# Even attention: the keys' low parts in four lasting tiles, written once each, with the other half of the rows zeroed one time

## The chip, the cores and the metric

The kernel runs on one core of one Trainium2 chip. The core has five engines, each with its own in-order instruction stream: TensorE (PE, matrix products into PSUM), VectorE (DVE), ScalarE (ACT), GpSimd (POOL) and SyncE (SP, which starts most of the transfers). Weight loads of TensorE are shown as PEld. The metric is the time of one execution on the device in microseconds (us); less is better.

## The reference

A two-layer block over 512 positions and 256 context positions with 1024 channels. Layer 0 (the "even" one, the place of the change) mixes a gated chunk MLP with a differential attention of four heads; layer 1 is a windowed attention; each is followed by a SwiGLU feed-forward. Cut to the even attention:

```python
def diff_attn(q, k, v, lam):
    b, tq = q.shape[0], q.shape[1]
    tk = k.shape[1]
    s = jnp.einsum('bqhd,bkhd->bhqk', q, k).astype(jnp.float32) * ATTN_SCALE
    p = jax.nn.softmax(s, axis=-1).reshape(b, B_HEADS, 2, tq, tk)
    a = p[:, :, 0] - lam * p[:, :, 1]
    return jnp.einsum('bhqk,bkhe->bqhe', a.astype(v.dtype), v)

# even_mixer: q, k are rotated (rope); keys and values of the context are appended
k_all = jnp.concatenate([k, kc], axis=1)      # 512 + 256 = 768 keys
o = lax.map(lambda qb: diff_attn(qb, k_all, v_all, lam), q_blocks)
oc = diff_attn(qc, kc, vvc, lam)              # context queries, context keys alone
```

Each of the four heads has two components of 64 channels (the softmaxes that are subtracted) and values of 128 channels.

## The kernel before

**Precision by parts.** TensorE multiplies here in the type fp32r. To come nearer to float32, a tensor is split: its high part is the value cast to fp32r, its low part is what is left (the value less the high part). A general product is then three matmuls (`mm3`, lines 115 to 117): high x high, high x low, low x high.

**Scores by stacking.** A component has 64 channels and TensorE contracts over 128 rows, so the scores do it in two matmuls instead of three. Call a half of the 128 rows X for one component (rows 0 to 63 for the first, 64 to 127 for the second) and the other half Y. `stack_q` makes for each component a tile of queries (`qa`, `qb`) with the high part in X and the low part in Y (lines 272, 273 on ACT; line 276 on DVE, on POOL for the last head). `stack_k` makes for each component two tiles of keys: `kh` has the high part in both halves (lines 287, 288 on ACT), `kl` has the low part in both halves (line 290 on DVE, once for X and once for Y). The query tile times `kh` gives high x high and low x high, the query tile times `kl` gives high x low and low x low (lines 553 and 554: 512 columns of the sequence, 256 of the context). All four key tiles of a head come from a ring of six buffers (tag "sk"), 128 x 768 in fp32r.

**Work of a head.** `head(t)` runs three pairs of query blocks (`attend`, qp 0 to 2; the last pair are the context's queries, which see 256 keys alone). For each block and component (`softmax_diff`): score product into a PSUM tile `pw` (two such tiles), DVE's maximum (line 555), ACT's exponential `e` with its sum (line 557), then on DVE the reciprocal (561), a factor (562), the difference of the two softmaxes (563) and a small row (564). Then TensorE transposes `e` (line 575), ACT casts the high part `ath` (131), DVE subtracts the low part `atl` (132), and `mm3` multiplies with the values; ACT copies the output (587). The next head's tiles (`stack(t + 1)`) are made after a head's second pair. The head's norm runs in three steps inside the next head (sums by line 165, small operations 144 to 148 and 176, diagonal matrices by line 185 multiplied at 195, then line 620).

**The rest of the stage.** Between the attention's steps TensorE has filler work: the gated projections `gated(i)`, into a PSUM tile `pf` by `mm3`, copied out by ACT (line 596), their weights cast by ACT (89) with the low part subtracted on POOL (92). After the first two heads come four gelus on ACT (line 643, here with a table load, and a second load for the exponentials after it), and per group transposes (655), copies (656) and statistics (659, 660).

**What sets the order.** The program is written by head and by group; a scheduler orders each engine's instructions by priority and by an estimate of when operands and buffers come free. Heads 2 and 3 have a raised priority. A different number of instructions or another buffer therefore changes the order on several engines, also of lines that the change doesn't touch. The order on each engine is then fixed; at run time an engine waits for the next instruction in its row.

## Time and profile before

| what | us |
|---|---|
| runs, median | 1572.99 |
| runs, lowest to highest | 1571.8 to 1576.91 |
| the profiled execution | 1574.88 |
| its span in the profile | 1573.0 |
| TensorE busy in the span | 1514.1 |
| VectorE busy | 1073.0 |
| GpSimd busy | 826.1 |
| ScalarE busy | 727.8 |
| mean granted clock of TensorE | 0.994 |

Times in the profile run from the start of its span. In a timeline row stand the start, the duration, the engine, the line of the kernel, the operation, what is written <- what is read, the shape, and in brackets the time for which the engine was idle just before and which engine's work ended that. The first attention, with the projections between, takes the stretch from about 157 to 350 us.

### The profile page before, as it was taken

Reading aid. Unit: us, or ns where it says so; the run is one execution under the profiler, and the core shown is the slowest. Engines: PE = TensorE matmul, PEld = TensorE weight load, DVE = VectorE, ACT = ScalarE, POOL = GpSimd, SP = SyncE. Lnnn points to the kernel's source line nnn. Section 1 sums busy time; section 2 is a strip of 40 time slices with the busy share of each in tenths; the row PEclk is TensorE's granted clock in tenths of the full one; section 3 lists DMA queues with packets and bytes.
Section 4 is the critical chain, followed back from the end, with each engine's and each line's share of the span. In section 5 each row is a group of like instructions: output and inputs, shape, how many; then the busy total and the mean of one; then the engine's idle time right before and its main releaser. Section 6 shows DMA issues by size and latency. Waiting matters only on the chain.

```text
span 1573.0 us, 24994 instructions
## 1 busy us (share of the span) xinstructions
PE 1514.1 (96%) x9563; PEld 1352.0 (86%) x9563; DVE 1073.0 (68%) x1938; ACT 727.8 (46%) x1490; POOL 826.1 (53%) x558
## 2 busy tenths in 40 slices
PE   6999987999999999999999999999999999999998
PEld 4776876889999999999999988777869889999997
DVE  3720788765697787888786486765667966666665
ACT  2422677553553333333333354555645644444444
POOL 0464211050347777777776544531314399898982
PEclk9999999999999999999999999999999999999999
DMA  9835100033223333344542212200224133333301
GB/s 331 311 131 201 45 8 1 1 134 134 68 74 121 114 95 128 128 150 165 167 157 85 79 47 61 68 28 15 68 95 173 54 104 103 104 100 108 95 21 54
DMA packets 53416, 162.26 MB, mean 103 GB/s; under 512 B 6193, under 2 KB 8625, under 8 KB 45617
## 3 DMA queue, kind: packets, MB, share of 16 engines
q1 hardware_dynamic: 46240, 135.37, 25.7%
q10 hardware_dynamic: 7056, 25.30, 5.0%
q8 instruction: 75, 1.23, 0.3%
q14 instruction: 45, 0.36, 0.1%
HBM read 158.55 MB, written 2.10 MB: 102 GB/s over the span
## 4 chain that ended last, share of the span: by engine, by line
PE 85%; DVE 10%; ACT 3%; issue 1%; DMA 0%; DVEq 0%; SPq 0%; ACTq 0%
PE pw L115 12%; PE pw L116 12%; PE pw L117 11%; PE pb L116 8%; PE pb L117 8%; PE pb L115 8%; PE pf L115 4%; PE pf L116 4%; PE pf L117 4%; PE pb L1635 2%; PE pb L1624 2%; PE pf L370 2%; PE pw L1586 1%; PE pw L1594 1%; DVE t L49 1%
## 5 line engine op out<-in xcount | busy, mean ns | idle before, releaser
L116 PE MATMUL pw<-ax,w 128*128 128x384 f32 (+2 forms) x740 | 237.0, 321 | 3.5 <-DVE ax L49 2.2
L115 PE MATMUL pw<-ax,w 128*128 128x384 f32 (+2 forms) x740 | 235.9, 321 | 3.6 <-DVE q L49 1.9
L117 PE MATMUL pw<-ax,w 128*128 128x384 f32 (+2 forms) x740 | 236.4, 320 | 0.1
L785 DVE SCALAR_TENSOR_TENSOR xT<-pb,mod,xT 128x512 f32<-128x512 f32 (+3 forms) x204 | 143.2, 708 | 129.3 <-PE pb L117 128.8
L92 POOL TENSOR_TENSOR w<-raw,w 128x512 fp32r<-128x512 f32 (+1 forms) x76 | 115.4, 1526 | 219.0 <-ACT w L89 196.3
L49 POOL TENSOR_TENSOR w<-raw,w 128x512 fp32r<-128x512 f32 x122 | 185.0, 1531 | 48.8 <-ACT w L49 48.7
L49 POOL TENSOR_TENSOR w<-t,w 128x512 fp32r<-128x512 f32 x99 | 148.7, 1505 | 55.7 <-ACT w L49 55.7
L115 PE MATMUL pb<-hh,w 128*128 128x512 f32 x480 | 171.4, 357 | 1.2 <-DVE xT L785 1.2
L117 PE MATMUL pb<-hh,w 128*128 128x512 f32 x480 | 171.7, 358 | 0.4 <-DVE w L49 0.4
L116 PE MATMUL pb<-hh,w 128*128 128x512 f32 x480 | 171.3, 357 | 0.0
L115 PE MATMUL pw<-T,w 128*128 128x384 f32 (+1 forms) x508 | 156.6, 310 | 2.5 <-DVE hs L991 1.2
L116 PE MATMUL pw<-T,w 128*128 128x384 f32 (+1 forms) x508 | 157.0, 310 | 1.2 <-DVE T L132 1.2
L117 PE MATMUL pw<-T,w 128*128 128x384 f32 (+1 forms) x508 | 157.0, 310 | 0.0
L116 PEld LDWEIGHTS pw<-ax,w 128*128 128x128 f32 x740 | 140.8, 190 | 10.4 <-DVE ax L477 3.1
L115 PEld LDWEIGHTS pw<-ax,w 128*128 128x128 f32 x740 | 140.0, 190 | 10.6 <-DVE q L49 2.7
L115 PE MATMUL pf<-ax,w 128*128 128x256 f32 (+2 forms) x428 | 140.7, 329 | 3.9 <-ACT f L596 2.8
L117 PEld LDWEIGHTS pw<-ax,w 128*128 128x128 f32 x740 | 140.7, 190 | 3.3 <-DVE w L954 0.4
L116 PE MATMUL pf<-ax,w 128*128 128x256 f32 (+2 forms) x428 | 139.6, 326 | 0.0
L117 PE MATMUL pf<-ax,w 128*128 128x256 f32 (+2 forms) x428 | 139.5, 326 | 0.0
L49 POOL TENSOR_TENSOR hh<-hs,hh 128x768 fp32r<-128x768 f32 (+1 forms) x42 | 77.3, 1842 | 94.7 <-ACT hh L49 70.7
L49 POOL TENSOR_TENSOR w<-rawo,w 128x512 fp32r<-128x512 f32 x59 | 103.8, 1759 | 28.6 <-ACT w L49 28.6
L240 DVE SCALAR_TENSOR_TENSOR junk<-ar,cb 128x1024 bf16<-128x1024 f32 x64 | 105.7, 1651 | 0.0
(412 smaller groups left out, 3909.2 us busy)
## 6 DMA issues: line engine op xcount, KB each, us to landing
raw<-ffn_in SPq DMA_DIRECT2D x44, 1024.0 KB, 5.1
ar<-ada SPq DMA_DIRECT2D x24, 1024.0 KB, 6.8
ar<-ada ACTq DMA_DIRECT2D x48, 512.0 KB, 3.6
rawo<-ffn_out SPq DMA_DIRECT2D x88, 256.0 KB, 3.0
raw<-odd_out SPq DMA_DIRECT2D x28, 256.0 KB, 2.7
raw<-qk SPq DMA_DIRECT2D x16, 256.0 KB, 7.9
raw<-uv SPq DMA_DIRECT2D x16, 256.0 KB, 2.7
raw<-even_out SPq DMA_DIRECT2D x8, 512.0 KB, 3.9
```

Source lines behind the costliest of these rows:

```text
L49: self.tail[key] = fn(*args, **kw)
L92: eng.tensor_tensor(lo, raw, hi.bitcast(F32), ALU.subtract)
L115: mm(out, s[0], m[0], start=start, stop=False, **kw)
L116: mm(out, s[0], m[1], start=False, stop=False, **kw)
L117: return mm(out, s[1], m[0], start=False, stop=stop, **kw)
L240: return self.nc.vector.scalar_tensor_tensor(junk, t, 1.0, self.cb[who], ALU.mult, ALU.mult, accum_out=self.acc[who][:, col:col + 1])
L370: nc.tensor.matmul(ps[32 * q:32 * q + 32, :w], cst[:, k, :], t[:, w * q:w * q + w], start=k == 0, stop=k == KT - 1, skip_group_check=True)
L785: ins = self.nc.vector.scalar_tensor_tensor(h, ps[:, r], self.modcol(l, j, m, who), h, ALU.mult, ALU.add)
L1586: nc.tensor.matmul(ps[:, st:en], Q, K[g][p][:, b0 * P:b1 * P], start=p == 0, stop=p == 1, skip_group_check=True)
L1594: last = nc.tensor.matmul(ps[:, en:en + TC], Q, K[g][p][:, TX:], start=p == 0 and not edge, stop=p == 1, skip_group_check=True)
L1624: last = nc.tensor.transpose(pt[:, x * P:(x + 1) * P], es[2 * (x % 2) + x // 2][:, kb * P:(kb + 1) * P], self.ident)
L1635: nc.tensor.matmul(po[64 * h:64 * h + 64, :], V[vb][:, 64 * g:64 * g + 64], t[:, h * TC:h * TC + TC], start=kb == 0, stop=kb == nb - 1, sk ...
```

## The change

`stack_k` no longer makes `kl` for itself. Four tiles for low parts are made once, two sets of two (one for each component); heads 0 and 2 use the first set, 1 and 3 the second. The half Y of each is set to zero on POOL once, before the first head; `stack_k` then has DVE write the low part to X alone. So eight of sixteen subtractions (line 290) are gone and four memsets of 64 x 768 are added. `kh` has a ring of three buffers of its own (tag "kh"). Of the score, the product low x low is no longer contained. The number and shapes of the matmuls are the same; the tiles take 3,072 bytes more of each partition (21,504 for 18,432).

```diff
-    def stack_k(self, k, pool, T, tag, bufs):
+    def stack_k(self, k, pool, T, tag, bufs, lows):
         nc = self.nc
         out = []
-        for X, Y in ((slice(0, 64), slice(64, 128)), (slice(64, 128), slice(0, 64))):
+        for X, Y, kl in zip((slice(0, 64), slice(64, 128)), (slice(64, 128), slice(0, 64)), lows):
             kh = pool.tile([P, T], F32R, name=self.uid("kh"), tag=tag, bufs=bufs)
-            kl = pool.tile([P, T], F32R, name=self.uid("kl"), tag=tag, bufs=bufs)
             nc.scalar.copy(kh[X], k[X])
             nc.scalar.copy(kh[Y], k[X])
-            for Z in (X, Y):
-                nc.vector.tensor_tensor(kl[Z], k[X], kh[X].bitcast(F32), ALU.subtract)
+            nc.vector.tensor_tensor(kl[X], k[X], kh[X].bitcast(F32), ALU.subtract)
             out.append((kh, kl))
         return out
@@
+        lows = [[Ra.tile([P, TA], F32R, name=f"kl{i}{c}") for c in range(2)] for i in range(2)]
+        for i in range(2):
+            nc.gpsimd.memset(lows[i][0][64:128].bitcast(F32), 0.0)
+            nc.gpsimd.memset(lows[i][1][0:64].bitcast(F32), 0.0)
+
         def stack(t):
             return (self.stack_q(qk[t], Ra, TA, "sq", 3, eng=nc.gpsimd if t == 3 else nc.vector),
-                    self.stack_k(qk[4 + t], Ra, TA, "sk", 6))
+                    self.stack_k(qk[4 + t], Ra, TA, "kh", 3, lows[t % 2]))
```

Lines 291 to 597 of before are two less in the changed kernel, those from 598 on three more. In what follows a name with a number is one buffer or one use of it. The order on POOL differs in the four memsets alone; on ACT, DVE and PE it differs inside the first attention, and is the same after it.

The first place is ACT while head 1's first context block is under way (before 196.68 to 203.58 us in the trace): `kh` with the numbers 1828 is head 2's key tile. Before:

```order
127 L287 CAST kh_1540<-f_105_578 64x768
128 L288 CAST kh_1540<-f_105_578 64x768
129 L273 ACTIVATE qb_1529<-f_103_574 64x768
130 L272 ACTIVATE qa_1822<-f_138_883 64x768
131 L557 ACTIVATE e_1571,sa_1566<-pw_1567,sa_1565 128x256
132 L557 ACTIVATE e_1577,sa_1566<-pw_1573,sa_1565 128x256
133 L131 CAST ath_1502<-pb_1497 128x512
134 L287 CAST kh_1828<-f_140_887 64x768
135 L288 CAST kh_1828<-f_140_887 64x768
136 L596 COPY f_368_2039<-pf_2040 128x512
```

After:

```order
127 L286 CAST kh_1542<-f_105_578 64x768
128 L287 CAST kh_1542<-f_105_578 64x768
129 L273 ACTIVATE qb_1533<-f_103_574 64x768
130 L286 CAST kh_1828<-f_140_887 64x768
131 L287 CAST kh_1828<-f_140_887 64x768
132 L272 ACTIVATE qa_1822<-f_138_883 64x768
133 L555 ACTIVATE e_1571,sa_1566<-pw_1567,sa_1565 128x256
134 L555 ACTIVATE e_1577,sa_1566<-pw_1573,sa_1565 128x256
135 L131 CAST ath_1506<-pb_1501 128x512
136 L594 COPY f_362_2035<-pf_2036 128x512
```

The two copies into `kh_1828` moved ahead of two exponentials.

The second place is PE in head 1's context pair (before about 227 to 229 us): the products of lines 553 and 554 into `pw`, and the last one that reads the first key tile of head 1, whose buffer head 2's second key tile takes. Before:

```order
948 L115 MATMUL pb_1651<-ath_1687,vhi_1290 128x256
949 L116 MATMUL pb_1651<-atl_1688,vhi_1290 128x256
950 L117 MATMUL pb_1651<-ath_1687,vlo_1291 128x256
951 L115 MATMUL pb_1651<-ath_1687,vhi_1294 128x256
952 L116 MATMUL pb_1651<-atl_1688,vhi_1294 128x256
953 L117 MATMUL pb_1651<-ath_1687,vlo_1295 128x256
954 L165 MATMUL pb_1705<-ones,sq_1601 128x128 x2
955 L575 MATMUL pb_1776<-ident_100,e_1737 128x128
956 L554 MATMUL pw_1854<-kh_1540,qb_1529 128x256
957 L554 MATMUL pw_1854<-kl_1541,qb_1529 128x256
958 L554 MATMUL pw_1867<-kh_1534,qa_1528 128x256
959 L554 MATMUL pw_1867<-kl_1535,qa_1528 128x256
```

After:

```order
948 L552 MATMUL pw_1850<-kh_1542,qb_1533 128x256
949 L552 MATMUL pw_1850<-kl_1323,qb_1533 128x256
950 L115 MATMUL pb_1651<-ath_1687,vhi_1290 128x256
951 L552 MATMUL pw_1863<-kh_1538,qa_1532 128x256
952 L552 MATMUL pw_1863<-kl_1322,qa_1532 128x256
953 L116 MATMUL pb_1651<-atl_1688,vhi_1290 128x256
954 L117 MATMUL pb_1651<-ath_1687,vlo_1291 128x256
955 L115 MATMUL pb_1651<-ath_1687,vhi_1294 128x256
956 L116 MATMUL pb_1651<-atl_1688,vhi_1294 128x256
957 L117 MATMUL pb_1651<-ath_1687,vlo_1295 128x256
958 L165 MATMUL pb_1705<-ones,sq_1601 128x128 x2
959 L573 MATMUL pb_1776<-ident_100,e_1737 128x128
```

The products `pw_1867` (now `pw_1863`) moved ahead of five products with the values, of the sums of line 165 and of one transpose.

The third place is PE at the first score products of head 3 (before about 272 to 276 us). Before:

```order
1138 L575 MATMUL pb_2347<-ident_100,e_2293 128x128
1139 L575 MATMUL pb_2347<-ident_100,e_2316 128x128
1140 L553 MATMUL pw_2471<-kh_2390,qb_2379 128x512
1141 L554 MATMUL pw_2471<-kh_2390,qb_2379 128x256
1142 L553 MATMUL pw_2471<-kl_2391,qb_2379 128x512
1143 L554 MATMUL pw_2471<-kl_2391,qb_2379 128x256
1144 L115 MATMUL pf_2896<-ax_311,w_2887 128x512
```

After:

```order
1137 L573 MATMUL pb_2343<-ident_100,e_2312 128x128
1138 L573 MATMUL pb_2343<-ident_100,e_2289 128x128
1139 L573 MATMUL pb_2343<-ident_100,e_2312 128x128
1140 L115 MATMUL pf_2888<-ax_311,w_2879 128x512
1141 L116 MATMUL pf_2888<-ax_312,w_2879 128x512
1142 L117 MATMUL pf_2888<-ax_311,w_2879 128x512
1143 L115 MATMUL pf_2888<-ax_313,w_2879 128x512
```

The filler into `pf_2896` (now `pf_2888`) stood behind the second component's score product; now sixteen of its matmuls stand ahead of it.

## Prediction

> **What bounds the kernel now.** I read the page's engine shares and the chain of work first, then a table by windows, then the waits and the timelines of TensorE (PE), VectorE (DVE) and ScalarE (ACT) where the table shows PE not full.
>
> ```profile
> PE 1514.1 (96%) x9563; PEld 1352.0 (86%) x9563; DVE 1073.0 (68%) x1938; ACT 727.8 (46%) x1490; POOL 826.1 (53%) x558
> PE 85%; DVE 10%; ACT 3%; issue 1%; DMA 0%; DVEq 0%; SPq 0%; ACTq 0%
> ```
>
> PE is the bound nearly everywhere. The change touches the first attention only, so the windows of that stage and of what follows count (window, its length, then busy time of PE, weight loads, DVE, ACT and GpSimd (POOL), granted clock, DMA):
>
> ```profile
> 150.00:350.00 200.00, 181.65 (x1099) 157.26 (x1098) 152.10 (x368) 127.51 (x244) 43.38 (x24) 0.97 0.12 38
> 350.00:425.00 75.00, 75.00 (x440) 74.17 (x438) 40.41 (x99) 31.95 (x68) 21.48 (x15) 1.00 0.31 108
> 225.00:250.00 25.00, 17.46 (x88) 13.82 (x87) 21.22 (x59) 19.29 (x35) 3.09 (x2) 0.80 0.00 0
> ```
>
> From 150 to 350 us PE is idle for 200 - 181.65 = 18.35 us; nothing that changes there can win more than that plus the slow clock. From 350 on PE is full, so what has been won or lost by then is carried to the end. The worst stretch is 225 to 250: PE idle for 7.5 us, DVE busy for 21.2 of 25, clock 0.80. The stretch after it, PE's largest wait (sum, times, longest), its stops (start, duration, in brackets the idle time before it and what ended that) and the clock:
>
> ```profile
> 250.00:275.00 25.00, 21.71 (x143) 19.39 (x144) 20.49 (x54) 17.57 (x39) 4.60 (x3) 1.00 0.00 1
> PE pw L553 <- ACT e L557: 6.5, 5, 1.8
> 200.61 0.50 PE L553 MATMUL pw<-kh,qa 128*128 128x512 f32 x1 [1.37 <-ACT e L557]
> 203.74 0.39 PE L115 MATMUL pf<-ax,w 128*128 128x256 f32 x1 [1.33 <-ACT f L596]
> 231.60 0.39 PE L554 MATMUL pw<-kh,qb 128*128 128x256 f32 x1 [2.51 <-ACT e L557]
> 241.94 0.47 PE L115 MATMUL pb<-ath,vhi 128*128 128x256 f32 x1 [1.54 <-ACT ath L131]
> 244.24 0.79 PE L553 MATMUL pw<-kh,qa 128*128 128x512 f32 x1 [1.84 <-ACT e L557]
> 271.77 0.47 PE L553 MATMUL pw<-kh,qa 128*128 128x512 f32 x1 [1.66 <-ACT e L557]
> 274.22 0.47 PE L553 MATMUL pw<-kh,qb 128*128 128x512 f32 x1 [0.96 <-ACT e L557]
> 314.69 0.38 PE L115 MATMUL pb<-ath,vhi 128*128 128x256 f32 x1 [0.73 <-ACT ath L131]
> 232.00:234.00 2.00, 1.91 (x7) 1.43 (x7) 1.97 (x8) 1.04 (x4) 0.00 (x0) 0.50 0.00 0
> 234.00:236.00 2.00, 2.00 (x12) 1.81 (x12) 2.00 (x8) 1.97 (x5) 0.00 (x0) 0.68 0.00 0
> 242.00:250.00 8.00, 5.88 (x22) 4.80 (x22) 6.43 (x18) 4.44 (x8) 0.00 (x0) 0.57 0.00 0
> ```
>
> A score product (lines 553 and 554) waits until the exponential (line 557) two products earlier has emptied its PSUM tile. That exponential waits for the DVE's maximum (line 555). So the loop is PE, DVE, ACT, PE, and whatever stands in the queues of DVE and ACT between two of its steps lengthens the stop. The stop of 2.51 us was followed by a clock of 0.50; that of 1.66 by none, the clock of 250 to 275 being 1.00.
>
> **What the removed work costs where it stands.**
>
> ```profile
> L290 DVE TENSOR_TENSOR kl<-f,kh x16: 942/954/1994, 158.0 to 270.2; 64x768 fp32r<-64x768 f32 x16
> 229.28 1.92 DVE L290 TENSOR_TENSOR kl<-f,kh 64x768 fp32r<-64x768 f32 x2
> 231.43 0.95 DVE L276 TENSOR_TENSOR qb<-f,qb 64x768 fp32r<-64x768 f32 x1
> 240.45 2.96 DVE L290 TENSOR_TENSOR kl<-f,kh 64x768 fp32r<-64x768 f32 x2 [0.91 <-ACT kh L287]
> 269.19 1.92 DVE L290 TENSOR_TENSOR kl<-f,kh 64x768 fp32r<-64x768 f32 x2
> 271.22 1.86 DVE L563 SCALAR_TENSOR_TENSOR e<-e,sa,e 128x256 f32<-128x256 f32 x1
> ```
>
> Eight of sixteen subtractions go: 8 x 0.954 = 7.6 us of DVE time. All on the path, that is the most it wins by itself. PE has as many matmuls as before, ACT as many copies. Part by part:
>
> *The first heads (157 to 170): 0.* Here stand three of the eight, and four new memsets on POOL.
>
> ```profile
> 161.94 1.96 POOL L92 TENSOR_TENSOR w<-raw,w 128x512 fp32r<-128x512 f32 x1 [6.21 <-ACT w L89]
> L354 POOL MEMSET cst<- 128x256 f32 x1 | 0.3, 315 | 0.0
> 169.00 0.50 PE L553 MATMUL pw<-kh,qa 128*128 128x512 f32 x1
> ```
>
> POOL stands idle for 6.21 us ahead of 161.94. A memset of 128x256 takes 0.315 us; in proportion to the elements of a row one of 64x768 takes 3 x 0.315 = 0.95, so four take at most 3.8 us by this estimate and end before 161.94. The first score product runs at 169.00 and is reached by PE in its order, without a stop, so neither the saving nor the memsets move it. Cover gone, the four would cost 3.8. The bounds are 0 and -0.15, for DVE's splits of v that come a little earlier.
>
> *196 to 206: +0.4.* The copies for head 2's first key pair (ACT 201.38 and 202.24) now stand ahead of the two exponentials that the stop at 200.61 waits for.
>
> ```profile
> 201.38 0.84 ACT L287 CAST kh<-f 64x768 fp32r<-64x768 f32 x1
> 202.24 0.83 ACT L288 CAST kh<-f 64x768 fp32r<-64x768 f32 x1
> 200.02 0.45 ACT L557 ACTIVATE e<-pw,sa 128x256 f32<-128x256 f32 x1
> ```
>
> That puts them 0.84 + 0.83 = 1.67 us later, and the stop grows from 1.37 to 3.04. The next stop, 1.33 us for the copy of line 596, was itself due to these two copies in front of it and mostly goes. Net +1.67 - 1.27 = +0.4 (a rest of 0.06 of that stop is my reading of the new order). Bounds: 0.3 (1.67 - 1.33), and 1.67 if that stop stays.
>
> *226 to 244: -2.3.*
>
> ```profile
> 228.41 0.83 ACT L287 CAST kh<-f 64x768 fp32r<-64x768 f32 x1 [0.47 <-PE pw L554]
> 230.99 0.47 ACT L557 ACTIVATE e<-pw,sa 128x256 f32<-128x256 f32 x1
> 232.99 0.47 ACT L557 ACTIVATE e<-pw,sa 128x256 f32<-128x256 f32 x1 [0.96 <-DVE sm L148]
> 234.04 0.48 ACT L557 ACTIVATE e<-pw,sa 128x256 f32<-128x256 f32 x1
> 234.63 1.28 ACT L643 ACT_TABLE_LOAD   x1
> 243.20 0.90 ACT L557 ACTIVATE e<-pw,sa 128x768 f32<-128x768 f32 x1
> ```
>
> Two things. First, the key copy at 228.41 waits for the last score product that reads the old buffer; in the new order this product stands ahead of seven other rows of PE and its exponential ahead of the output copy, so key copies and the exponential at 230.99 come earlier: by my walk along the new rows 1.3 us, at least the copy's wait of 0.47 and at most the walk. Secondly, DVE has one subtraction less (0.95) between 229.28 and the maxima that the exponentials at 232.99 and 234.04 wait for. Both act in series up to the table load at 234.63; from there ACT runs through the four gelus, the key copies and the second table load to the exponential at 243.20, which releases the product at 244.24. Work in that piece is the same but for the copy of line 131 that now stands between the gelus. So 244.24 comes 1.3 + 0.95 = 2.25, some 2.3 us earlier, bounds 0.47 and 2.6. The subtraction saved at 240.45 is worth nothing: its keys are wanted after 270.
>
> *The clock after that: -1.3.* In 242 to 250 the clock of 0.57 cost PE 0.43 x 5.88 = 2.5 us. The stops ahead of it (1.54 and 1.84) shrink, since in the new order 244.24's predecessors are drawn together, but filler (the gated projections) is still missing there. Bounds 0 and -2.5; I take the middle, as no row tells them apart.
>
> *268 to 275: -1.0.* One subtraction of 269.19 goes from in front of the maximum that the stop at 274.22 (0.96) depends on, and a block of sixteen filler matmuls, which before stood behind that product, now stands ahead of it: the stop goes. That at 271.77 (1.66) stays: ACT's copies, not DVE, are late there. Bounds 0 and -1.0 - 1.66 = -2.6.
>
> *275 to 350: +0.5.* The splits of line 132 change places with line 563 and with line 555; one of them comes later by one of each. The combine and the reduction of 768:
>
> ```profile
> 293.06 1.01 DVE L563 SCALAR_TENSOR_TENSOR e<-e,sa,e 128x768 f32<-128x768 f32 x1
> 293.99 0.95 DVE L555 TENSOR_REDUCE sa<-pw 128x1 f32<-128x768 f32 x1
> ```
>
> Their sum, 1.96, less some 0.4 us of other products still to run, is a new stop of up to 1.6. Against that the stop at 314.69 (0.73) can go. Bounds -0.7 and +1.6; I take +0.5, in the middle.
>
> *Sum:* 0 + 0.4 - 2.3 - 1.3 - 1.0 + 0.5 = -3.7 us. The profiled run took 1574.88 us (its span 1573.0 and 1.88 around it), 1.9 above the median of 1572.99. So 1571.2 on its own footing, and against the median 1572.99 - 3.7 = 1569.3, which is 0.24% less. The bound of what a measurement of this kernel can tell from no change is 0.3%, 4.7 us: the forecast lies just inside it.
>
> **Rivals.**
> *All of it on the path.* Each stop of 225 to 275 ends at a DVE step, and DVE is busy for 21.2 of 25 us there. If all eight subtractions count, -7.6, and with the clock's 2.5 about -10: 1563 to 1565. Against it: three of the eight stand under a full PE at 157 to 170.
>
> *Nothing.* Every row that ends a stop names ACT (e, f, ath), and ACT's work is unchanged; then the DVE saving becomes idle time there and the moved rows cancel: 0 to -1, so 1572 to 1573. Against it: ACT itself waits for DVE at 232.99 (0.96).
>
> *Slower, by the copies ahead of the exponentials at 200.* It decides where the new stop exceeds the 2.51 us after which the clock was 0.50, while that of 1.66 at 271.77 left it at 1.00. At 3.04 it does, if nothing fills it. Price: 1.67 for the late exponentials, the clock over the next 4 us as in 232 to 236 (2 x 0.50 + 2 x 0.32 = 1.6), and the new stop of 1.6 near 295, with filler spent early so that nothing is won back between: +4.9, about 1578. Against it: the projections that follow 203.74 wait for the same queue and would start sooner.
>
> [...]
>
> *Slower, by the memsets.* DVE and POOL slow each other: the longest subtraction, 1.994 against 0.942, lies beside the POOL work at 161.94. Four memsets beside DVE's queue at 156 to 160 add up to 4 x (1.994 - 0.942) = 4.2 us to a DVE queue that is relieved there by 3 x 0.954 = 2.9, so +1.3 at most, and only if it reaches 169.00: 1574.3. [...]
>
> **How the numbers follow.** Forecast, -2 to -6: 0.50, of which 0.22 lies beyond 4.7 us. All on the path: 0.20. Nothing: 0.10. Slower by the copies: 0.18, by the memsets and what else: 0.02. Faster by over 0.3%: 0.22 + 0.20 = 0.42; within: 0.28 + 0.10 = 0.38; slower: 0.20 (a chance given to the whole of those cases, as starved stops tend to add). The range runs from 1564 (most of the first rival) to 1578 (the price of the slower one); what lies outside is part of each, under 0.2 together. The likeliest case alone has 1567 to 1571.
>
> **What would show it.** In the changed profile: eight subtractions of about 0.95; four memsets ended before 169; the stop at 200.6 near 3 us and none near 203.7; the table load near 232.5 and the score product of 244.24 near 242.3; no stop at the place of 274.22; a clock above 0.57 in what was 242 to 250; full PE after 350. I am wrong if the stop at 200 halves the clock, if the table load stays near 234.6, or if the filler that now runs early opens a gap in 206 to 226 or after 275 larger than 1.6 us.

## The result and the profile after

The changed kernel is slower, by little. Its median is 1577.57 us (15 executions, 1575.49 to 1581.35), that of the kernel before, measured with it, 1575.4 (15, 1571.8 to 1577.17); the ratio is 1.0018, 95% interval 1.0011 to 1.0026, that is 1.7 to 4.1 us. The forecast was 3.7 us faster. The time lies inside the range that was given; its sign is the other one, and so many executions resolve 0.08%, not the 0.3% that the text took for the bound.

The page's shares and its chain of work, of the changed kernel (1575.49 us in the profiled execution, span 1573.7):

```profile
PE 1513.0 (96%) x9563; PEld 1352.1 (86%) x9563; DVE 1069.2 (68%) x1930; ACT 728.4 (46%) x1490; POOL 829.8 (53%) x562
PE 84%; DVE 10%; ACT 3%; issue 2%; DMA 0%; POOL 0%; DVEq 0%; SPq 0%; ACTq 0%; POOLq 0%
```

DVE has eight instructions less, POOL four more; nothing else moved at this level. The windows (window, length, then PE, weight loads, DVE, ACT and POOL busy, granted clock, DMA) of the changed kernel:

```profile
150.00:350.00 200.00, 180.26 (x1089) 157.14 (x1089) 144.59 (x360) 125.45 (x242) 44.78 (x28) 0.97 0.11 37
350.00:425.00 75.00, 75.00 (x442) 74.25 (x441) 40.89 (x94) 31.85 (x65) 22.83 (x15) 1.00 0.32 112
225.00:250.00 25.00, 16.97 (x95) 14.05 (x94) 20.84 (x60) 19.32 (x35) 2.65 (x2) 0.86 0.00 0
```

DVE has 152.10 - 144.59 = 7.5 us less to do in the first attention, as forecast, and less of PE's work falls inside the window, not more: 180.26 us for 181.65. PE is full from 350 us on, as before.

To compare kernels I measure one stretch: from ACT's first exponential of a score of 768 to its first cast of line 131 into `ax`, when the attention is over. Such rows of the kernel before:

```profile
171.00 0.90 ACT L557 ACTIVATE e<-pw,sa 128x768 f32<-128x768 f32 x1 [1.33 <-DVE sa L555]
...
325.73 2.30 ACT L131 CAST ax<-o 128x768 fp32r<-128x768 f32 x3 [0.59 <-PE pf L116]
```

and of the changed one:

```profile
171.14 0.91 ACT L555 ACTIVATE e<-pw,sa 128x768 f32<-128x768 f32 x1 [1.05 <-DVE sa L553]
...
327.14 2.31 ACT L131 CAST ax<-o 128x768 fp32r<-128x768 f32 x3 [0.59 <-PE pf L116]
```

The stage takes 325.73 - 171.00 = 154.73 us before and 327.14 - 171.14 = 156.00 after: 1.27 longer. Where, PE's stops show (timeline of the changed kernel):

```profile
202.45 0.79 PE L551 MATMUL pw<-kh,qa 128*128 128x512 f32 x1 [3.08 <-ACT e L555]
...
227.38 0.39 PE L116 MATMUL pb<-atl,vhi 128*128 128x256 f32 x1 [1.50 <-DVE atl L132]
...
233.24 0.39 PE L552 MATMUL pw<-kh,qb 128*128 128x256 f32 x1 [2.03 <-DVE qb L276]
...
244.37 0.80 PE L551 MATMUL pw<-kh,qa 128*128 128x512 f32 x1 [3.14 <-ACT e L555]
...
253.76 0.40 PE L115 MATMUL pf<-ax,w 128*128 128x512 f32 x1
...
272.39 0.47 PE L551 MATMUL pw<-kh,qa 128*128 128x512 f32 x1 [1.68 <-ACT e L555]
...
297.31 0.39 PE L116 MATMUL pb<-atl,vhi 128*128 128x256 f32 x1 [1.37 <-DVE atl L132]
...
316.09 0.38 PE L115 MATMUL pb<-ath,vhi 128*128 128x256 f32 x1 [0.73 <-ACT ath L131]
```

The stop at 200.6 has grown from 1.37 to 3.08, and that at 244 from 1.84 to 3.14; those of 1.50 and 1.37 are new. The stop of 0.96 at 274.22 is gone. The filler product at 253.76 ends the stretch behind the stop of 3.14; its row in the kernel before (needed below):

```profile
253.07 0.48 PE L115 MATMUL pf<-ax,w 128*128 128x512 f32 x1
```

The clock, windows of the changed kernel:

```profile
202.00:204.00 2.00, 1.55 (x5) 1.36 (x6) 1.93 (x6) 2.00 (x7) 0.00 (x0) 0.55 0.06 12
204.00:206.00 2.00, 2.00 (x11) 1.81 (x11) 2.00 (x5) 0.94 (x2) 0.00 (x0) 0.60 0.00 0
242.00:250.00 8.00, 5.63 (x20) 5.07 (x21) 5.62 (x17) 5.11 (x10) 0.37 (x1) 0.57 0.00 0
```

It is halved behind the stop of 3.08 and behind that of 3.14.

### The profile page after: what moved, and what is told of

It is laid out like the page before. It is cut to its first block, busy times and chain, and to the rows that moved or that the text cites. A ratio compares the mean times of both kernels' runs of the same rounds, so it can differ in the third digit from the quotient of the medians.

```text
span 1573.7 us, 24993 instructions
## 1 busy us (share of the span) xinstructions
PE 1513.0 (96%) x9563; PEld 1352.1 (86%) x9563; DVE 1069.2 (68%) x1930; ACT 728.4 (46%) x1490; POOL 829.8 (53%) x562
## 4 chain that ended last, share of the span: by engine, by line
PE 84%; DVE 10%; ACT 3%; issue 2%; DMA 0%; POOL 0%; DVEq 0%; SPq 0%; ACTq 0%; POOLq 0%
PE pw L115 12%; PE pw L116 11%; PE pw L117 11%; PE pb L116 8%; PE pb L117 8%; PE pb L115 8%; PE pf L115 4%; PE pf L116 4%; PE pf L117 4%; PE pb L1638 2%; PE pb L1627 2%; PE pf L368 2%; PE pw L1589 1%; PE pw L1597 1%; DVE t L49 1%
```

## Experiments

Two things came together in this change: less work for DVE, and another order on PE, ACT and DVE, because the scheduler answered to that. To hold the order fixed, the kernels marked "pinned" take each engine's order from a table of runs of instruction numbers, as dependencies that only order (no semaphore is added):

```python
for e, runs in ORDER.items():
    mine = [i for i in nc.cur_bb.bb.instructions if i.engine == getattr(mybir.EngineType, e)]
    row = [mine[k] for s, n in runs for k in range(s, s + n)]
    for p, i in zip(row, row[1:]):
        tc.add_manual_dep(i, p.name, NO_SYNC, reason="order")
```

What was measured; the stage is the stretch defined above, from one profiled execution of each kernel, against 154.73; the ratio is of timed executions, to the kernel before:

| kernel | subtractions | first exponential, cast into ax | stage | ratio, 95% |
|---|---|---|---|---|
| the changed kernel | 8 | 171.14, 327.14 | 156.00 (+1.27) | 1.0018 [1.0011, 1.0026] |
| new_work_old_order | 8 | 170.58, 323.91 | 153.33 (-1.40) | 0.9994 [0.9982, 1.0007] |
| old_work_new_order | 16 | 171.74, 329.09 | 157.35 (+2.62) | 1.0041 [1.0026, 1.0056] |
| ring_zeroed_each_time | 8 | 170.08, 326.26 | 156.18 (+1.45) | 1.0012 [1.0000, 1.0023] |
| keys_behind_exponentials | 8 | 170.48, 322.41 | 151.93 (-2.80) | 0.9996 [0.9986, 1.0006] |
| old_work_third_order | 16 | 171.82, 325.84 | 154.02 (-0.71) | 1.0015 [1.0004, 1.0027] |
| old_work_keys_ahead | 16 | 171.25, 327.62 | 156.37 (+1.64) | 1.0019 [1.0004, 1.0033] |
| keys_back_alone | 8 | 172.76, 326.82 | 154.06 (-0.67) | 1.0010 [0.9999, 1.0022] |
| keys_back_splits_early | 8 | 172.17, 326.53 | 154.36 (-0.37) | 0.9992 [0.9983, 1.0001] |
| stop_filled | 8 | 170.43, 325.83 | 155.40 (+0.67) | 1.0019 [1.0008, 1.0029] |
| keys_of_head3_late | 8 | 170.91, 321.79 | 150.88 (-3.85) | 0.9985 [0.9974, 0.9995] |
| keys_late_split_early | 8 | 170.72, 320.90 | 150.18 (-4.55) | 0.9977 [0.9964, 0.9989] |

Timed ratios lie on average 0.1% (1.6 us) above what the stage alone gives; what that may be stands in the last section. The readings rest on the stage; the two agree on which kernels are at the ends. One trace of each kernel is enough for this as long as the clock does the same: exponential by exponential, kernels of the same order lie within 0.03 us of each other up to the edit or to the first place where the clock of one execution is halved and that of the other is not. From there such a stretch shifts one against the other, by up to 1.04 us (ring_zeroed_each_time beside the changed kernel, 211 to 245 us).

**The work and the order apart.** new_work_old_order is the changed kernel, pinned to the order of before, without the eight subtractions that are gone. old_work_new_order is the kernel before (all sixteen subtractions, each second one right behind the first), pinned to the order of after.

```diff
+    pin(tc.nc, tc)   # changed kernel: order of before; kernel before: order of after
```

> The changed kernel (eight subtractions, four memsets, lasting tiles) with its instructions on TensorE, VectorE and ScalarE held in the order that the kernel before has. Theory (the new order costs time, the removed subtractions win some): 1.5 to 3 us under the kernel before, with the stop of 2.51 us at the score product of 231.60 shortened by about 0.95. Rival (the removed subtractions lie under other work, as ScalarE ends every stop): within 0.7 us of the kernel before. Rival (something in the new tiles or the memsets costs time, not the order): about 2.8 us over the kernel before, like the changed kernel.

> The kernel before (sixteen subtractions, no memsets) with its instructions held in the order of the changed kernel, each second subtraction right behind its first. Theory: the order's loss without the gain, 1.5 to 3 us slower than the changed kernel, so about +4.5 to +6 against the kernel before. Rival (subtractions under other work): like the changed kernel, about +2.8. Rival (tiles or memsets): like the kernel before, within 0.7 us.

In the old order the eight subtractions are worth 1.40 us; in the new order 157.35 - 156.00 = 1.35. The new order costs 2.62 with the old work and 156.00 - 153.33 = 2.67 with the new. The two add up: -1.40 + 2.67 = +1.27. So the change's own work makes the attention shorter, and the order that comes with it makes it longer by twice as much. Within each order both kernels have their halved clock at the same places (232 and 242 us in the old order, 202 to 203 and 243 to 244 in the new), so the clock is not in the 1.40 and 1.35. The timed runs agree on the order, by intervals that don't meet (1.0011 to 1.0026 for the changed kernel, 0.9982 to 1.0007 for its work in the old order); that the work wins anything in the old order they don't show. Both effects are smaller than was expected: 1.40 for 1.5 to 3, with the stop of 2.51 not shortened at all (2.53), and +2.62 for +4.5 to +6 (timed: +4.1 to +8.8).

Rows of new_work_old_order, from the timelines of DVE, ACT and PE, in this order:

```profile
230.60 0.95 DVE L276 TENSOR_TENSOR qb<-f,qb 64x768 fp32r<-64x768 f32 x1 [0.56 <-ACT qb L273]
233.95 1.28 ACT L646 ACT_TABLE_LOAD   x1
231.21 0.39 PE L552 MATMUL pw<-kh,qb 128*128 128x256 f32 x1 [2.53 <-ACT e L555]
271.14 0.47 PE L551 MATMUL pw<-kh,qa 128*128 128x512 f32 x1 [1.66 <-ACT e L555]
```

The table load comes 233.95 - 170.58 = 63.37 us after the first exponential, before it was 234.63 - 171.00 = 63.63: one subtraction of 0.95 less in series is worth 0.26 there, since DVE now waits 0.56 for ACT's query tile. At the product of 271.14 the gain is still no more than 0.21 (100.56 for 100.77); the other 1.2 of the 1.40 comes behind it, where the stop of 0.96 at 274.22 is gone from the timeline. In the new order, too, 0.87 of the 1.35 comes there, between the exponentials at 271.68 and 276.01 of the changed kernel. So in both orders most of what the eight are worth arises behind one of them, that of head 3's keys near 270.

**The tiles.** ring_zeroed_each_time is the kernel before with one edit; its order, made by the scheduler alone, is that of after on PE, ACT and DVE.

```diff
-            for Z in (X, Y):
-                nc.vector.tensor_tensor(kl[Z], k[X], kh[X].bitcast(F32), ALU.subtract)
+            nc.gpsimd.memset(kl[Y].bitcast(F32), 0.0)
+            nc.vector.tensor_tensor(kl[X], k[X], kh[X].bitcast(F32), ALU.subtract)
```

> The kernel before with one edit: GpSimd writes the zero half of each low-part tile each time (eight memsets) and VectorE only the other half; no lasting tiles. Its order on TensorE, ScalarE and VectorE is that of the changed kernel. Theory (order and subtractions alone): the time of the changed kernel within 0.7 us, about +2.8 against the kernel before. Rival (the lasting tiles matter): within 0.7 us of the kernel before. Rival (memsets cost): slower than the changed kernel by up to 3 us, as four more of 0.74 us stand beside VectorE's work.

Eight memsets in a ring or four in tiles that stay: 0.18 us apart, in the stage. That this is so little is in part luck: the exponentials of the two lie within 0.01 us up to 207 us; then the clock is halved for 6.8 us in this execution for 3.4 in the other, which puts it 1.04 behind; after 245 us it is the changed kernel's clock that is halved for longer (6.8 us for 3.4), which makes most of that good. Up to where the clocks part, that the tiles last is worth nothing. The scheduler chooses this order without them; whether for the missing subtractions or for the memsets in their place, no run tells apart.

**A third order.** The two exponentials at 200.02 and 200.47 that the copies moved ahead of are those of head 0's context pair, its last two (the text ahead of the prediction calls the place head 1's). keys_behind_exponentials is the changed kernel with head 2's key copies tied behind head 0's last exponential; the scheduler orders the rest anew. old_work_third_order is the kernel before, pinned to that order.

```diff
+            with self.tc.issue_after(behind.ins) if behind else ExitStack():
-            nc.scalar.copy(kh[X], k[X])
-            nc.scalar.copy(kh[Y], k[X])
+                nc.scalar.copy(kh[X], k[X])
+                nc.scalar.copy(kh[Y], k[X])
```

> The changed kernel with head 2's key copies on ScalarE held behind head 0's last exponential, as they stood before the change; the scheduler orders the rest. Theory 1 (the stop of 3.08 us at 202.45 and the half clock after it are the loss): that stop back to about 1.4 us, no clock of 0.5 in 202 to 206, and about 1.8 us less than the changed kernel, or +1 against the kernel before. Theory 2 (the loss is the filler that is spent early and the VectorE wait of 1.5 us at 227.38): the time stays that of the changed kernel, +2.8 against the kernel before.

The copies go back to their place behind the two exponentials, and other rows move too. The stop (timeline of PE):

```profile
200.07 0.50 PE L552 MATMUL pw<-kh,qa 128*128 128x512 f32 x1 [1.35 <-ACT e L556]
```

It has the old size, and the stage is 2.80 us shorter than before, and 4.07 shorter than the changed kernel's, where the theory had 1.8: the rest is the other rows. The timed ratio (0.9986 to 1.0006) doesn't tell this kernel from the one before.

> The kernel before (sixteen subtractions) in the order of the kernel whose key copies are held behind the exponentials. In the stage that kernel took 162.6 us. Theory (order and subtractions add, the eight subtractions are 1.5 us as in the two orders measured): 164.1 us in the stage, 1.4 under the kernel before, though no work is removed. Rival (the third order is good only because the subtractions are gone): as long as the kernel before, 165.5, or longer.

In this order the eight subtractions are worth 154.02 - 151.93 = 2.09, more than in the other two. The reason is seen on PE, in stops for the norm's diagonal matrices and output, of old_work_third_order:

```profile
239.06 1.10 PE L195 MATMUL pb<-q,ones 128*128 128x512 f32 x2 [2.11 <-DVE q L185]
...
243.59 1.22 PE L195 MATMUL pb<-q,ones 128*128 128x256 f32 x2 [2.15 <-DVE o L620]
```

They end on DVE; in keys_behind_exponentials they are 1.69 and 0.63. Of the 2.09, 0.93 arises there; 0.87 comes behind 270, as in the other orders. What the eight are worth depends on the order around them: 1.40, 1.35 and 2.09 us in the three.

**The key copies alone.** old_work_keys_ahead is the kernel before, pinned to its own order but for this move on ACT; keys_back_alone is the changed kernel with the move undone (and the subtraction that reads those copies put later on DVE).

```diff
+CAST kh_1828<-f_140_887 64x768
+CAST kh_1828<-f_140_887 64x768
 ACTIVATE qa_1822<-f_138_883 64x768
 ACTIVATE e_1571,sa_1566<-pw_1567,sa_1565 128x256
 ACTIVATE e_1577,sa_1566<-pw_1573,sa_1565 128x256
 CAST ath_1502<-pb_1497 128x512
-CAST kh_1828<-f_140_887 64x768
-CAST kh_1828<-f_140_887 64x768
```

> The kernel before with its own order on every engine but for one move: on ScalarE head 2's two key copies (201.38 and 202.24) stand ahead of the query copy and of the two exponentials at 200.02 and 200.47, as in the changed kernel. Measured by the time from the first score product to the end of the stage (first matmul of the output product into pb after 330 us; 165.5 us in the kernel before). Theory (this move is most of the order's loss of 2.65 us): the stop at 200.61 grows to about 3.05 us and the clock falls to 0.5 for one window behind it; the stage is 1 to 2.5 us longer. Rival (the filler and VectorE's rows make the loss, this move is made up by the next stop, as the prediction had it with +0.4): at most 0.5 us longer.

> The changed kernel with its own order on every engine but for that move undone: the two key copies go back behind the two exponentials and the cast after them, and on VectorE the subtraction that needs them goes behind the second maximum after that. Theory: the stop at 202.45 back to about 1.4 us, full clock, the stage 1 to 2.5 us shorter than in the changed kernel (166.7 us). Rival: at most 0.5 us shorter, and what the kernel with the keys held behind the exponentials won came from the rest of its order.

Done alone the move costs 1.64 us of the stage; undone alone it gives back 156.00 - 154.06 = 1.94. The stop and the clock, in old_work_keys_ahead:

```profile
202.53 0.50 PE L553 MATMUL pw<-kh,qa 128*128 128x512 f32 x1 [3.05 <-ACT e L557]
...
202.00:204.00 2.00, 1.47 (x5) 1.32 (x6) 1.29 (x4) 2.00 (x8) 0.00 (x0) 0.73 0.01 4
204.00:206.00 2.00, 2.00 (x9) 1.82 (x8) 2.00 (x3) 1.35 (x3) 0.00 (x0) 0.50 0.03 8
```

This is the single largest piece of the order's 2.65: 1.6 to 1.9. At the place itself both ways give 1.6; the other 0.3 of the second arises behind 245 us, where the halved stretches of the two executions lie differently.

**The clock at that stop.** stop_filled keeps the order of after, with the four transposes ahead of the stop repeated, 28 in all for 4, so that PE is busy while it waits. The repeats write what the first ones wrote.

```diff
-                for j in range(2):
+                for j in [0, 1] * (7 if (t, qp, i) == (0, 1, 4) else 1):
```

> The changed kernel in its own order, with the four transposes that end before the stop at 202.45 done seven times instead of once: 24 more matmuls of about 0.12 us (2.8 us in all) into the same PSUM tile with the same values, so TensorE is busy in the stop of 3.08 us and nothing that follows can start sooner for it. The stage is measured on ScalarE, from the first exponential (171.14) to the first cast of line 131 into ax (327.14): 156.0 us in the changed kernel. Theory (the stop brings one window of half clock, and that is most of what the late exponentials cost): no clock of 0.5 in 202 to 206, the copy of line 594 at 203.22 waited for by TensorE again, and the stage 0.7 to 1.6 us shorter though work is added. Rival (the lateness is the cost, the clock is not): within 0.3 us of 156.0. Rival (the repeats delay the cast after them): longer.

Rows of its PE timeline and the clock's windows:

```profile
198.06 3.22 PE L573 MATMUL pb<-ident,e 128*128 128x128 f32 x28
201.73 0.50 PE L551 MATMUL pw<-kh,qa 128*128 128x512 f32 x1 [0.46 <-ACT e L555]
...
202.00:204.00 2.00, 2.00 (x15) 1.82 (x15) 1.93 (x7) 1.56 (x5) 0.00 (x0) 1.00 0.00 0
204.00:206.00 2.00, 2.00 (x19) 2.00 (x19) 2.00 (x4) 0.99 (x2) 0.00 (x0) 1.00 0.00 0
```

The exponentials are as late as in the changed kernel (201.73 - 170.43 = 31.30 for 202.45 - 171.14 = 31.31), yet the clock stays at 1.00, and the stage is 156.00 - 155.40 = 0.60 shorter. Where the halved clock acts, filling the stop wins more: the first filler product behind it, of the changed kernel and of stop_filled, is 34.25 and 32.93 us after the first exponential.

```profile
205.39 0.39 PE L115 MATMUL pf<-ax,w 128*128 128x256 f32 x1
```

```profile
203.36 0.28 PE L115 MATMUL pf<-ax,w 128*128 128x256 f32 x1
```

These 1.32 are 1.43 by 206 us, nearly all of the move's 1.6. Then 0.60 is lost by 214, with a stop of 0.36 for a split of line 132 at 210.10 that the changed kernel doesn't have, and 0.28 at 232, where this execution's clock was halved behind a stop of 2.02 (0.71 over 230 to 234) and the changed kernel's was not (1.00). So at the stop the move's cost is mostly the halved clock: with the clock whole, the later exponentials alone put that product 0.19 behind its place in the kernel before (203.74 - 171.00 = 32.74). How much of it reaches the end of the stage depends on the waits that follow: 0.60 here, a little under the 0.7 that the theory had. The timed ratio (1.0019) doesn't show those 0.6.

**The new stops at splits.** keys_back_splits_early is keys_back_alone with two splits of line 132 put ahead of the maximum that stood before each on DVE.

```diff
+TENSOR_TENSOR atl_1673<-pb_1667,ath_1672 128x512
 TENSOR_REDUCE sa_1752<-pw_1762 128x1
-TENSOR_TENSOR atl_1673<-pb_1667,ath_1672 128x512
...
+TENSOR_TENSOR atl_2521<-pb_2515,ath_2520 128x512
 TENSOR_REDUCE sa_2600<-pw_2610 128x1
-TENSOR_TENSOR atl_2521<-pb_2515,ath_2520 128x512
```

> The kernel with the key copies put back alone (stage 154.06 us from the first exponential to the first cast into ax, 0.73 more than the changed work in the old order, 153.33), and on VectorE two splits of line 132 that TensorE waits for moved ahead of the maximum before them: that of the stop of 1.50 us at 227.42 and that of the stop of 1.36 us at 297.06. Theory (the rest of the order's loss is these two stops): each 0.6 to 0.9 us shorter, the stage 0.7 to 1.8 us shorter, 152.3 to 153.4. Rival (the maximum that is late by 0.68 passes it on to the next exponential, and the rest lies elsewhere): within 0.3 us of 154.06.

The two stops, of 1.50 and 1.36 in keys_back_alone, shrank:

```profile
226.36 0.39 PE L116 MATMUL pb<-atl,vhi 128*128 128x256 f32 x1 [0.63 <-DVE atl L132]
...
296.48 0.39 PE L116 MATMUL pb<-atl,vhi 128*128 128x256 f32 x1 [0.36 <-DVE atl L132]
```

but the stage did not: 154.36 for 154.06. A part of that is the clock: with the same order of PE and ACT up to there, and the same stop of 1.36 at the score product, this execution's clock was halved behind it, and the other's was not. Windows of keys_back_splits_early, and then of keys_back_alone:

```profile
202.00:204.00 2.00, 2.00 (x8) 1.67 (x8) 1.93 (x7) 1.99 (x5) 0.00 (x0) 0.57 0.04 8
```

```profile
202.00:204.00 2.00, 1.65 (x9) 1.40 (x9) 1.93 (x6) 1.99 (x7) 0.00 (x0) 1.00 0.01 4
```

The next stop, 1.34 us in keys_back_alone, took up most of it (0.38 there), and 0.39 is left at the exponentials up to 222 us. The exponential at 227.26, whose maximum now stands behind the first split, adds 0.60 to that, of which 0.4 stays: here the rival was right. Behind the second split 0.71 is won: here the theory was, and keys_late_split_early, below, wins 0.70 by the same move. So the split's stop near 297 is worth about as much as the 0.73 that keys_back_alone still took more than the same work in the old order; that this difference is that stop and nothing else is not shown.

**A faster version.** keys_of_head3_late takes the third order and moves head 3's query copy and first two key copies, which stood on ACT between the two table loads, behind the first two exponentials after the second load; the DVE subtraction that reads them follows, and one later exponential goes ahead of a copy. keys_late_split_early moves one split as well, the second of those just shown.

```diff
-ACTIVATE qa_2374<-f_139_885 64x768
-CAST kh_2380<-f_141_889 64x768
-CAST kh_2380<-f_141_889 64x768
 CAST ath_1811<-pb_1806 128x512
 ACT_TABLE_LOAD
 ACTIVATE e_2165,sa_2158<-pw_2159,sa_2157 128x768
 COPY f_348_1909<-pf_2770 128x512
 ACTIVATE e_2173,sa_2158<-pw_2167,sa_2157 128x768
+ACTIVATE qa_2374<-f_139_885 64x768
+CAST kh_2380<-f_141_889 64x768
+CAST kh_2380<-f_141_889 64x768
```

> The changed kernel in that third order with two more moves on ScalarE, and one on VectorE that goes with the first: head 3's query copy and first two key copies stand behind the first two exponentials after the second table load, not ahead of that load; and the first exponential that head 3's first score product waits for stands ahead of the second key copy of head 3's second component. Theory (what stands ahead of an exponential for which TensorE waits is what costs): the score product at 241.5 up to 2.4 us earlier, the stop of 1.66 us at 267.66 gone, in the stage 2 to 4 us less than 162.6. Rival (the next wait takes it: VectorE's diagonal matrices, and the second exponential): within 0.7 us of 162.6.

ACT's two table loads, of keys_of_head3_late:

```profile
232.31 1.28 ACT L646 ACT_TABLE_LOAD   x1
...
237.13 1.28 ACT L555 ACT_TABLE_LOAD   x1
```

They are 4.82 us apart, for 7.27 in keys_behind_exponentials (231.93 and 239.20), and the stage is 151.93 - 150.88 = 1.05 shorter, between the rival's 0.7 and the theory's 2. The exponential behind the second load comes 2.50 earlier, the one at 246.30 only 1.10: 1.4 is lost in between, as the rival said: the diagonal product at 239.67 still waits 0.63 for DVE (line 623) and comes only 1.21 earlier. The stop of 1.66 at 267.66, which the theory wanted gone, is one of 1.71 for a cast of line 131 at 267.76 instead.

> The kernel with head 3's keys late, and one more move: on VectorE the split of line 132 that TensorE waited 1.36 us for at 291.96 stands ahead of the maximum before it (0.92 us) and of what follows that. Its stage took 150.9 us (from the first exponential to the first cast into ax). Theory (a VectorE row in front of what TensorE waits for is worth its length there, as the eight subtractions were): 0.5 to 0.9 us less. Rival (the maximum is now late by 0.68 and the next exponential with it): no change within 0.3 us.

The split's stop went from 1.36 to 0.36, and the stage is 0.70 shorter. It is won at the split: the exponentials up to 267.60 lie within 0.1 us of those of keys_of_head3_late, though the clock behind the table loads was halved for 3.4 us here and for 6.8 there. The PE timeline and the attention's window, of keys_late_split_early:

```profile
290.78 0.39 PE L116 MATMUL pb<-atl,vhi 128*128 128x256 f32 x1 [0.36 <-DVE atl L132]
...
150.00:350.00 200.00, 184.42 (x1128) 160.71 (x1127) 144.22 (x362) 130.63 (x248) 50.25 (x30) 0.99 0.12 39
```

This is the fastest of all: median 1571.87 us (8 executions) beside 1575.4 (18) of the kernel before on the same chip, ratio 0.9977 [0.9964, 0.9989]. It beats the kernel before by 2 to 6 us, and with it the changed one, which is slower than that. The work is that of the change; only the order is another.

## Why the prediction was wrong

For each step I compare the place of the same product relative to the first exponential (171.00 and 171.14). The difference of those differences is what the step brought. Work that the order moved across such a product is counted where it now stands, so the single steps are less sure than their sum.

| stretch, up to the product at (before, after) | forecast | measured |
|---|---|---|
| first heads | 0 | +0.14, ahead of the stage |
| 196 to 206: 200.61, 202.45 | +0.4 | +1.70 |
| 226 to 244: 244.24, 244.37 | -2.3 | -1.71 |
| the clock after that: 253.07, 253.76 | -1.3 | +0.56 |
| 253 to 272: 271.77, 272.39 | not in the sum | -0.07 |
| 272 to the end: 325.73, 327.14 | -1.0 + 0.5 | +0.79 |
| sum in the stage | -3.7 | +1.27 |

*First heads: right for this pair.* In the kernel before, DVE waited 0.46 for PE ahead of the first maximum, in the changed one 1.97, so the saving there became idle time. (In two of the four kernels with sixteen subtractions, old_work_new_order and old_work_third_order, the first score product waits 0.46 and 0.44 for DVE, in none of the nine with eight; the stage begins behind that.) The memsets are shorter than estimated (0.74 us, not 0.95). From the groups of instructions by line, changed kernel (durations lowest, median, highest in ns):

```profile
L599 POOL MEMSET kl<- x2: 736/736/737, 156.2 to 157.8; 64x768 f32 x2
L288 DVE TENSOR_TENSOR kl<-f,kh x8: 949/956/1990, 158.5 to 269.8; 64x768 fp32r<-64x768 f32 x8
```

The rival of the memsets falls with it: DVE's subtraction at 158.48, beside two of them, took 0.95 as elsewhere. The prediction had also misread its longest subtraction: that of 1.99 us stands at 240.45, beside a row of POOL of 1.80 at 239.83, and the one beside POOL's row at 161.94 took 1.76. That DVE and POOL slow each other was not tested by itself; of POOL's 72 rows of line 92 and 128x512 in the kernel before, the 20 with no row of DVE beside them took 1.26 to 1.30, the other 52 1.27 to 2.08, that at 161.94 1.96.

*196 to 206, +0.4: this step failed.* The copies stand where the forecast put them, and the stop grew as it said, to 3.08 for 3.04 (ACT of the changed kernel):

```profile
199.39 0.83 ACT L286 CAST kh<-f 64x768 fp32r<-64x768 f32 x1
...
201.85 0.45 ACT L555 ACTIVATE e<-pw,sa 128x256 f32<-128x256 f32 x1
```

What it set against that, 1.27 from the next stop, did go as a stop, but came back as a clock of 0.55 to 0.60 over the same products: the first filler product behind (203.74, 205.39) is still 1.51 late, and the next ones 1.66. With the clock at 1.00, in stop_filled, it is 0.19 late, so the sum's +0.4 would have been about right; the term that it put at nothing is the halved clock, 1.3 to 1.4 at this place. The row that decides, the stop of 2.51 followed by a clock of 0.50, was quoted in the prediction, and the forecast kept the halved clock for a rival of 0.18. Measured apart, the move costs 1.64 to 1.94 instead of 0.4. That rival had the right row, a stop of 3.08 with a halved clock behind it, though a length of over 2.51 is not what separates the stops here (last section); its price of 4.9 was too high: its late exponentials and slow clock, 3.3 together, measured 1.6 to 1.9, as the stop of 1.33 went, and its new stop near 295, 1.6, was worth 0.7.

*226 to 244, -2.3: direction right, size off.* In place of the two gains in series, 1.71, which makes good the 1.70 lost before and no more. The second gain (0.95 for a subtraction) came in this order: old_work_new_order, with the subtraction, has its table load 64.55 us after its first exponential, the changed kernel 63.74; the 0.81 between them is also there at the product of 244.37. In the old order the subtraction gave 0.26, because the next work on DVE then waited for ACT. It is the first gain, 1.3, that was mis-sized. The key copy, the exponential behind the copies and the table load, of ACT in the changed kernel, and then the load of old_work_new_order:

```profile
229.64 0.83 ACT L286 CAST kh<-f 64x768 fp32r<-64x768 f32 x1 [0.65 <-PE pw L552]
...
232.62 0.47 ACT L555 ACTIVATE e<-pw,sa 128x256 f32<-128x256 f32 x1
...
234.88 1.28 ACT L646 ACT_TABLE_LOAD   x1
```

```profile
236.29 1.28 ACT L643 ACT_TABLE_LOAD   x1
```

Counted from the first exponential, the copy starts 1.09 later than before (228.41) and the exponential 1.49 later (230.99); the load, forecast near 232.5, is 0.11 late. The copy still waits for a product of PE, 0.65 for 0.47, and that product stands behind a new stop of 1.50 at 227.38. DVE's row ahead of that stop is this:

```profile
222.84 1.86 DVE L561 SCALAR_TENSOR_TENSOR e<-e,sa,e 128x768 f32<-128x768 f32 x1
224.62 1.24 DVE L562 SCALAR_TENSOR_TENSOR sx<-sa 128x1 f32<-128x1 f32 x1
225.78 0.94 DVE L553 TENSOR_REDUCE sa<-pw 128x1 f32<-128x768 f32 x1
226.65 0.67 DVE L132 TENSOR_TENSOR atl<-pb,ath 128x512 fp32r<-128x512 f32 x1
```

The split that PE waits for stands behind a maximum of 0.94. The forecast looked for such a stop only after 275.

*The clock after that, -1.3: this step failed, and by most.* It counted on the stops ahead of 244 to shrink. They were drawn together into one of 3.14, behind which the clock was 0.57 over 242 to 250 as before, and the filler product that ends the stretch comes 0.56 later than it did. The text named the missing filler there and still took half of the gain.

*272 to the end, -0.5 in sum: +0.79.* The stop at 274.22 is gone, as forecast, and new_work_old_order shows that this was worth some 1.2 with the order held. The split's new stop of 1.37 at 297.31, foreseen as up to 1.6 and taken at half with its counterweight, weighs more; that of 0.73 at 314.69 stayed (0.73 at 316.09) where it might have gone.

*Rivals.* All on the path: fell; eight subtractions are worth 1.35 to 2.09 of their 7.6, by the order. Nothing: fell, though the sum came near it; its premise, that every row that ends a stop names ACT, also missed one in the kernel before, of 1.10 at 239.30, which DVE ends (line 185). Slower by the copies: its place, its stop and its clock are there, at a third of its price in the stage. So the misjudged thing was not what the removed work is worth so much as what the order costs, 2.65, against which the forecast's own terms for moved rows (+0.4, -1.3, -1.3 and +0.5) stood at a gain of 1.7.

## What to carry to other kernels

Where a scheduler sets the order, an edit that takes work from one engine is two changes: hold the order fixed and measure the work, hold the work and measure the order. Copies that nothing needs soon, placed ahead of an exponential that TensorE waits for, made a stop of 3.08 us here for one of 1.37, and the costly part of it was the halved clock that followed (1.3 to 1.4 us of 1.6 to 1.9): ask of a stop how little TensorE does around it, and not only how long it is. When work has been removed, look for the order that suits what is left: here the same work ran the attention in 156.0 or in 150.2 us.

## What the runs showed of the hardware

*The clock.* In the clock records of these traces every halved stretch ahead of the program's last few us is 3.4 or 6.8 us long, and the distances between them in one execution are multiples of 3.41 (before: 231.85, 242.09, 975.96 and 1262.68, the later ones 3, 218 and 302 times 3.413 behind the first). A stop of 3.05 to 3.08 us near 202 came with one in each of the four kernels that had it. One of 1.36 came with one in keys_back_splits_early and not in keys_back_alone (the windows above). So the length of a stop by itself does not decide here. A count over the traces separates the cases: cut each execution between 150 and 350 us into the windows of 3.41 us that its halved stretches lie on, and take PE's busy time (as the profile models it) in each window at full clock. In the 13 traces, all 22 windows in which PE was busy for 12 to 48% were followed by a halved one, of 16 between 49 and 53% one was, and of 690 above none. So what goes with a halved stretch in these traces is how little PE did in the 3.41 us ahead of it, and these windows lie elsewhere in each execution: ahead of the stretch at 202.20 of the changed kernel PE was busy for 0.58 us of 3.41, ahead of that in keys_back_splits_early for 1.80, and the same stop in keys_back_alone fell across two windows of 2.22 and 1.77.

Outside the attention the number of such stretches ahead of the last few us differs from one profiled execution to another: two before, one after, none in keys_late_split_early, two to four in the others. One of them, in the kernel before:

```profile
1262.00:1266.00 4.00, 3.81 (x16) 3.52 (x17) 3.90 (x6) 0.37 (x1) 4.00 (x4) 0.58 0.37 82
```

and the same place in the changed kernel:

```profile
1262.00:1266.00 4.00, 2.12 (x15) 2.04 (x16) 3.90 (x5) 1.47 (x3) 4.00 (x4) 1.00 0.41 115
```

The changed kernel was 1.69 us behind there, relative to the start of the span, and 0.15 after it. A single execution therefore says nothing about 0.1%. Whether such stretches are also why the timed ratios lie 0.1% above the stage's differences is open: the timed executions have no trace.

*A small row beside GpSimd.* Line 562 on DVE, one element for each partition, took 1.24 us at 224.62 and 0.15 at 229.90. POOL in the changed kernel:

```profile
224.26 1.58 POOL L92 TENSOR_TENSOR w<-raw,w 128x512 fp32r<-128x512 f32 x1 [0.38 <-ACT w L89]
```

The slow row lies beside this one, which ends at 225.84, and DVE's next begins at 225.78; likewise the combine at 222.84, beside the POOL row before it, took 1.86 for 1.01. The 13 traces have 312 rows like this small one: the 36 that took over 0.3 us all overlap a subtraction of POOL, 271 overlap none, and five overlap one and are short. That POOL is the cause was not tested by itself.
